# Eighteen weight units instead of seventeen held ahead of an expert stage, and tokens gathered in plain fp32

## The chip, the cores and the metric

The kernel runs on one core of one Trainium2 chip. The metric is the device time of one launch in microseconds (us), the median of three runs. Engines are named as in the profile: PE (TensorE matmul), PEld (its weight loads), DVE (VectorE), ACT (ScalarE), POOL (GpSimd) and SP (SyncE, which here issues the weight DMAs).

## What is computed

Two transformer blocks over 256 tokens of width 1024. The first has a linear recurrence mixer, an attention mixer and two feed-forward layers; the second has two attentions, an output projection and a mixture of experts. Only the last part matters here:

```python
x = x + g1[:, None, :] * (merged @ w_out[l])
h2 = rmsnorm(x, norm2_g[l]) * (1.0 + sc2[:, None, :]) + sh2[:, None, :]
y_ffn = hierarchical_moe(h2, ...)   # 4 groups of 8 experts, the 2 best of one group per token
x = x + g2[:, None, :] * y_ffn
return rmsnorm(x, final_g)
```

Each of the 32 experts has a gate and an up matrix of 1024x512 and a down matrix of 512x1024, all fp32: 6 MB an expert, 192 MB in all.

## The kernel before

**Tiling.** The 256 tokens lie in two tiles of 128 (`t` = 0, 1). Weights come in units of 1 MB; `Stream` (class at L68) issues their DMAs on SP in the order of use into a pool of 17 ring tiles (`RING`). A unit can be loaded only when the matmuls on the unit that had its ring tile before are done. In the early layers a unit is split into a high and a low fp32r part, so that it holds three ring tiles; expert units are used raw, as plain fp32, and hold one. When the last split (of the output projection `bo`) is issued, `ahead` becomes `RING` and the expert units run as far ahead as tiles come free.

**Output projection and router.** `out_proj("bo", ...)` makes four sums `acc[t][nh]` (token tile, half of the columns). For each one `after_mix` adds it to the residual `xres` and sums its squares, and one tick later `later()` transposes it on PE (`pT`), scales it on DVE (`hg`) and multiplies it by the router's weights (`lg`, 8 PE records). Once both halves of a token tile are there, `route(t)` finds group and experts with a chain of small DVE instructions. Also there, `xrH` and `xrL`, the normed tokens as a high and a low fp32r part of 1024 columns, are made with ACT, DVE (t = 0) and POOL (t = 1). They fill four tiles of the `t4` pool (8 tiles of 128x1024). `warm(n)` are n PE matmuls whose result nobody reads. After the last `route`, `pos` (PE) counts places, `place` (DVE) is the slot of each token in its experts, and `selection(m)` writes a 0/1 matrix `sel` for four experts of 64 slots each.

**Gather.** `gathered(sel, half)` fetches the tokens of four experts by matmul: for each of four column chunks four fp32r matmuls of 256 columns (high and low part, two token tiles). Two evictions per PSUM tile, on DVE and on ACT, apply scale and shift and give `xs`.

**Expert loop.** `q` runs over 16 pairs of experts. The unit order is gate 0, up 0, gate 1, down 0, up 1, gate 2, down 1, up 2 and so on, four units each, so that unit numbers 0 to 191 follow from it: unit 17 is the second of up 1, unit 20 the first of gate 2, unit 37 the second of down 2. `half_in` multiplies two units (one for each expert of the pair), which run side by side on two column halves of PE; both become free at its end. `down_products(q-1)` stands between gate q and up q, `scatter` (`comb`) returns results to the residual. A selection serves two pairs; at odd q one half is gathered ahead of up q and one at the end (at q = 3 both at the end). At the end of even q, `places` makes `sT` from `sel` and from the token weights `wtr`. `token_weights()` (softmax over groups and experts, on ACT and DVE) is written at the end of q = 0; the scheduler of the tile library may move instructions ahead within an engine unless they are pinned (`k.pin`, `keep_in_program_order`).

Of the kernel before, what the change touches and what calls it, by code (L numbers as in the profile page):

```python
# [65 lines left out]


class Stream:  # L68

    def __init__(self, k, units):
        self.k = k
        self.units = units
        self.raws = {}
        self.parts = {}
        self.loaded = 0
        self.done = 0
        self.pos = 0
        self.ahead = AHEAD  # L80
        self.most = 2
        self.end = 2 * max(i + 1 for i, u in enumerate(units) if u[4])
        self.plan = []
        self.gated = {}

    def load(self, upto):
        k = self.k
        while self.loaded < min(upto, len(self.units)):
            name, srcs, kc, cols, _ = self.units[self.loaded]
            t = k.big(F32, f"w{self.loaded}")  # L90
            v = t[:, : kc * cols].rearrange("p (k n) -> p k n", k=kc)
            for k0, k1, ap in srcs:
                k.nc.sync.dma_start(v[:, k0:k1, :], ap)
            self.raws[self.loaded] = v
            self.loaded += 1

    def pump(self, upto=None):
# [5 lines left out]
        while self.pos < min(end, 2 * len(self.units)) and (upto is not None or n < self.most):  # L103
# [20 lines left out]
            if self.pos == self.end:  # L124
                self.ahead = RING
                self.load(self.done + self.ahead)
# [310 lines left out]
def two_blocks_kernel(ctx, tc, A, out, stop=None):  # L437
# [66 lines left out]

    def out_proj(prefix, yT, each):

        acc = [[None, None], [None, None]]
        for nh in range(2):
            W = st.take(f"{prefix}0{nh}")
            for t in range(2):  # L510
                acc[t][nh] = k.ps("acc")
                k.tok_mm(acc[t][nh], yT, range(4), t, W, True, False)
                tick()
        Ws = [st.take(f"{prefix}1{nh}") for nh in range(2)]
        for t in range(2):
            for nh in range(2):
                k.tok_mm(acc[t][nh], yT, range(4, 8), t, Ws[nh], False, True)
                each(t, nh, acc[t][nh])
                tick()
# [626 lines left out]
    def merged_T(nh, t, m):  # L1146
        pT = k.ps("mT")
        for i in range(4):
            nc.tensor.transpose(pT[:, i * P : (i + 1) * P], m[:, i * P : (i + 1) * P], k.ident)
# [28 lines left out]
    k.row("b_router", br)  # L1178
    xrH, xrL = ([k.t4(F32R, "xr" + n) for t in range(2)] for n in "HL")
    sh2 = modT[:, 24:32]  # L1180
# [56 lines left out]
    def after_mix(t, nh, p):  # L1237
# [10 lines left out]
        def later():  # L1248
            pT = k.ps("pT")
            for i in range(4):  # L1250
                c = 4 * nh + i
                nc.tensor.transpose(pT[:, i * P : (i + 1) * P], xres[:, t, c * P : (c + 1) * P], k.ident)
            hg, g = k.t2(name="hg"), geff[2][:, 4 * nh : 4 * nh + 4]
# [3 lines left out]
            if nh == 0:  # L1257
                lT[t] = k.ps("lg")
            else:
                xv = xres[:, t, :].rearrange("p (n c) -> p c n", c=8)  # L1260
                hv, lv = (x[t].rearrange("p (c n) -> p c n", c=8) for x in (xrH, xrL))
                nc.scalar.activation(hv, xv, AF.Copy, scale=r)
                if t == 0:
                    nc.vector.scalar_tensor_tensor(lv, xv, r, hv.bitcast(F32), op0=ALU.mult, op1=ALU.subtract)
                    yield 1
                else:
                    warm(5)
                    xn = k.t4(name="xn")
                    nv = xn.rearrange("p (c n) -> p c n", c=8)
                    for h in range(2):  # L1270
                        c = slice(4 * h, 4 * h + 4)
                        nc.scalar.activation(nv[:, c], xv[:, c], AF.Copy, scale=r)
                        nc.gpsimd.tensor_tensor(lv[:, c], nv[:, c], hv[:, c].bitcast(F32), op=ALU.subtract)
            pl = lT[t]
# [9 lines left out]

        routed.append(spawn(later(), 1))

    out_proj("bo", mT, after_mix)
    if stop == "mix2":
# [21 lines left out]
    def token_weights():  # L1310

        ng, gs, ejunk, e1, den, w1 = cut(2), cut(2), cut(2, 4), cut(2), cut(2), cut(2)
        nc.vector.tensor_scalar(ng, gtop[:, :, 0], -1.0, None, op0=ALU.mult)
        for t in range(2):
            nc.scalar.activation(ejunk[:, t, :], lg[:, t, 0:4], AF.Exp, bias=ng[:, t : t + 1], accum_out=gs[:, t : t + 1])
        nc.vector.tensor_tensor(e1, etop[:, :, 1], etop[:, :, 0], op=ALU.subtract)
        nc.scalar.activation(e1, e1, AF.Exp)
        nc.vector.scalar_tensor_tensor(den, e1, 1.0, gs, op0=ALU.add, op1=ALU.mult)
# [19 lines left out]
    def selection(m):  # L1338
# [6 lines left out]
        return sel  # L1345

    def gathered(sel, half):

        xs = k.t4(name="xs").rearrange("p (c s) -> p c s", c=4)
        for c2 in range(2):  # L1350
            p = k.ps("xs")
            for i in range(2):
                c = 4 * half + 2 * c2 + i
                n = 0
                for x in (xrH, xrL):
                    for t in range(2):
                        k.mm(p[:, i * 256 : (i + 1) * 256], x[t][:, c * P : (c + 1) * P], sel[:, t], i == 0 and n == 0, i == 1 and n == 3, True)
                        n += 1
            for i in range(2):
                c = 4 * half + 2 * c2 + i  # L1360
                pv, o = p[:, i * 256 : (i + 1) * 256], xs[:, 2 * c2 + i, :]
                if i:
                    nc.scalar.activation(o, pv, AF.Identity, scale=geffP[:, c : c + 1], bias=shP[:, c : c + 1])  # L1363
                else:
                    nc.vector.tensor_scalar(o, pv, geffP[:, c : c + 1], shP[:, c : c + 1], op0=ALU.mult, op1=ALU.add)  # L1365
        return xs

    def places(q, sel):
# [128 lines left out]
    def overflow():  # L1497
# [10 lines left out]
        for c in range(8):  # L1508
            for t in range(2):
                for h, x in enumerate((xrH, xrL)):  # L1510
                    k.mm(pT[:, t * P : (t + 1) * P], x[t][:, c * P : (c + 1) * P], conr("ident"), t == 0 and h == 0, t == 1 and h == 1, True)
            nc.vector.tensor_scalar(h2T[c // 4][:, c % 4, :], pT[:, 0:256], geffP[:, c : c + 1], shP[:, c : c + 1], op0=ALU.mult, op1=ALU.add)
# [173 lines left out]
```

## Time and profile before

| | |
|---|---|
| median of 3 runs | 1266.68 us (1266.67 to 1267.15) |
| the profiled execution, its own time | 1267.75 us |
| its span | 1266.1 us |
| PE busy | 1225.0 us (97%) |
| DVE, ACT, POOL busy | 719.3, 493.1, 74.7 us |
| HBM traffic | 362.96 MB, mean 287 GB/s |

A busy share of PE here counts matmuls as pipelined, with modelled ends, so 97% doesn't say that PE was the bound everywhere. The span in 40 slices, each of 31.65 us, tells two regimes apart: up to slice 25 the DMA rate wanders between 115 and 319 GB/s, and from slice 26 on (822.9 us) it stands at 420 to 422 GB/s until the last slice.

### The profile page before, as it was taken

How to read it: one execution, taken by the hardware profiler on the slowest of the kernel's cores; microseconds unless marked ns; L12 is line 12 of the kernel's file. 1: busy time of each engine (PE TensorE's matmuls, PEld its weight loads, DVE VectorE, ACT ScalarE, POOL GpSimd, SP SyncE). 2: the span in 40 equal slices, each digit the busy share in tenths (PEclk: the TensorE clock that was granted, in tenths of full speed). 3: DMA queues.
4: the chain of work that ended last, by engine and by line, in shares of the span. 5: the costliest groups of instructions: out<-in, count | busy, mean ns of one | idle time of the engine just before them, and what ended most of it. 6: DMA issues, size and time to landing. Idle time of an engine off the chain costs nothing. (4 is left out here: it accounts for less than half of the span.)

```text
span 1266.1 us, 15923 instructions
## 1 busy us (share of the span) xinstructions
PE 1225.0 (97%) x6247; PEld 852.3 (67%) x6247; DVE 719.3 (57%) x1188; ACT 493.1 (39%) x847; POOL 74.7 (6%) x94
## 2 busy tenths in 40 slices
PE   6999999999999999999999999999999999998996
PEld 6988888998897888898777887543444444343432
DVE  6888669766565866977877785322333322222233
ACT  6956535445676643445566632310110101010101
POOL 4000000000131000100100100000000000000001
PEclk9999999999999999999999999999999999999999
DMA  9756686774334878765635557799999999999995
GB/s 319 262 200 233 235 303 241 244 241 151 117 134 167 282 241 290 237 229 170 218 115 172 188 207 304 286 421 421 420 421 421 421 421 420 422 421 421 421 420 211
DMA packets 121951, 362.96 MB, mean 287 GB/s; under 512 B 6289, under 2 KB 33681, under 8 KB 97809
## 3 DMA queue, kind: packets, MB, share of 16 engines
q1 hardware_dynamic: 121584, 361.39, 75.5%
q8 instruction: 50, 0.82, 0.3%
q10 hardware_dynamic: 288, 0.52, 0.1%
q14 instruction: 29, 0.23, 0.0%
HBM read 360.84 MB, written 1.05 MB: 286 GB/s over the span
## 5 line engine op out<-in xcount | busy, mean ns | idle before, releaser
L242 PE MATMUL down<-w,hidT 128*64 128x512 f32 x512 | 123.1, 595 | 9.5 <-DMA w<-in_w_down_dram 9.5
L242 PE MATMUL up<-w,xs 128*64 128x512 f32 x512 | 122.4, 597 | 5.1 <-DMA w<-in_w_up_dram 5.0
L242 PE MATMUL gate<-w,xs 128*64 128x512 f32 x512 | 116.7, 598 | 0.0
L1424 DVE SCALAR_TENSOR_TENSOR down<-down,wsl,g 128x512 f32<-128x512 f32 x30 | 22.8, 759 | 145.3 <-PE down L242 143.7
L242 PEld LDWEIGHTS down<-w,hidT 128*64 128x64 f32 x512 | 41.4, 137 | 84.9 <-issue 59.6
L242 PEld LDWEIGHTS up<-w,xs 128*64 128x64 f32 x512 | 39.4, 136 | 72.8 <-issue 58.4
L1569 ACT ACTIVATE hid<-gate 128x512 f32<-128x512 f32 x16 | 9.6, 597 | 180.8 <-PE gate L242 180.8
L242 PEld LDWEIGHTS gate<-w,xs 128*64 128x64 f32 x512 | 34.0, 136 | 59.8 <-issue 58.1
L523 DVE TENSOR_TENSOR xres<-comb,xres 128x512 f32<-128x512 f32 x64 | 41.3, 686 | 44.8 <-PE comb L242 44.8
L710 DVE SCALAR_TENSOR_TENSOR adacc<-w,csil,adacc 128x512 f32<-128x512 f32 x84 | 65.2, 777 | 1.3
L1425 ACT CAST oH<-down 128x512 fp32r<-128x512 f32 x30 | 17.6, 587 | 123.7 <-DVE down L1424 123.7
L1363 ACT ACTIVATE xs<-xs,modP,geffP 128x256 f32<-128x256 f32 x32 | 18.1, 564 | 80.4 <-DVE xs L1365 80.4
L1582 DVE TENSOR_TENSOR hid<-up,hid 128x512 f32<-128x512 f32 x16 | 11.1, 692 | 63.8 <-PE up L242 50.4
L778 DVE SCALAR_TENSOR_TENSOR sg<-tb,rs,sg 128x512 f32<-128x512 f32 (+1 forms) x24 | 16.9, 705 | 52.1 <-PE tb L242 52.1
L1405 DVE COPY hidT<-hidT 128x512 f32<-128x512 f32 x16 | 11.1, 692 | 53.1 <-PE hidT L245 53.1
L269 ACT ACTIVATE junk<-xres 128x512 f32<-128x512 f32 x28 | 17.7, 631 | 55.0 <-DVE xres L523 52.7
L714 POOL TENSOR_TENSOR adL<-adacc,adH 128x512 fp32r<-128x512 f32 x12 | 20.0, 1666 | 311.0 <-ACT adH L713 311.0
L764 ACT CAST hH<-hT 128x512 fp32r<-128x512 f32 (+1 forms) x24 | 13.2, 551 | 46.2 <-PE hT L761 46.1
L242 PE MATMUL xs<-sel,xrH 128*128 128x256 f32 x128 | 27.7, 297 | 2.9 <-DVE sel L1342 2.5
L523 DVE TENSOR_TENSOR xres<-acc,xres 128x512 f32<-128x512 f32 x20 | 13.8, 691 | 28.8 <-PE acc L242 28.8
L242 PEld LDWEIGHTS comb<-oH,sT 128*128 128x128 f32 x62 | 11.6, 187 | 26.6 <-issue 24.3
L1479 POOL TENSOR_TENSOR out<-xres,fg 128x512 f32<-128x512 f32 x2 | 2.5, 1272 | 454.5 <-DVE xres L523 454.5
(1270 smaller groups left out, 3367.0 us busy)
## 6 DMA issues: line engine op xcount, KB each, us to landing
w<-in_w_gate_dram SPq DMA_DIRECT2D x64, 1024.0 KB, 19.8
w<-in_w_up_dram SPq DMA_DIRECT2D x64, 1024.0 KB, 19.8
w<-in_w_down_dram SPq DMA_DIRECT2D x60, 1024.0 KB, 19.8
w<-in_ffn_w_in_dram SPq DMA_DIRECT2D x32, 1024.0 KB, 6.6
w<-in_w_ada_dram SPq DMA_DIRECT2D x24, 1024.0 KB, 5.1
w<-in_w_in_dram SPq DMA_DIRECT2D x20, 1024.0 KB, 5.0
w<-in_ffn_w_out_dram SPq DMA_DIRECT2D x16, 1024.0 KB, 6.6
w<-in_ffn_w_in_dram SPq DMA_DIRECT2D x16, 768.0 KB, 5.4
```

Of the source, the lines that this page charges most:

```text
L242: self.pinned(self.nc.tensor.matmul(out, lhsT, rhs, start=start, stop=stop, skip_group_check=skip))
L269: self.nc.scalar.activation(junk[:, : src.shape[-1]], src, AF.Square, scale=scale, accum_out=acc)
L523: nc.vector.tensor_tensor(xres[:, t, s], p, xres[:, t, s], op=ALU.add)
L710: nc.vector.scalar_tensor_tensor(acc, raws[kh][:, i, :], c, acc, op0=ALU.mult, op1=ALU.add)
L714: nc.gpsimd.tensor_tensor(aL, acc, aH.bitcast(F32), op=ALU.subtract)
L764: nc.scalar.copy(hv, pv)
L778: nc.vector.scalar_tensor_tensor(h, p[:, :fw], rs[t], h, op0=ALU.mult, op1=ALU.mult)
L1363: nc.scalar.activation(o, pv, AF.Identity, scale=geffP[:, c : c + 1], bias=shP[:, c : c + 1])
L1405: nc.vector.tensor_copy(hT, p)
L1424: nc.vector.scalar_tensor_tensor(p, p, ws, gates["g2"][:, s], op0=ALU.mult, op1=ALU.mult)
L1425: nc.scalar.copy(oH, p)
L1582: nc.vector.tensor_tensor(hv, hidden_order(q, p), hv, op=ALU.mult)
```

## The change

It does five things.

1. `xrH` and `xrL` and the instructions that made them are gone. The first gather reads `xres` itself, with a selection `selr` that is scaled by each token's reciprocal norm; the later ones read `xc`, an fp32 copy of the scaled tokens, made by two ACT instructions of 1024 columns. Both are plain fp32 matmuls, half as many as before.
2. The first gather is cut by pair: `first_gathered(0)` fetches only the 128 slots of pair 0 ahead of gate 0, `first_gathered(1)` those of pair 1 between gate 0 and up 0.
3. The token tiles freed take an eighteenth expert unit: unit 17 goes into two `t4` tiles (`Halves`) instead of a ring tile, once.
4. The router is pinned in written order (`k.pin` set before `out_proj("bo")`, transposes by `k.turn`), the second half of that projection is cut into pieces of two chunks, and `later()` runs two ticks after its sum. `warm` ahead of the last router product is 2 instead of 5.
5. The start of `token_weights()` is pinned, so that it can't be moved ahead.

```diff
@@ class Stream
+        self.spare = self.end // 2 + RING
+            if self.loaded == self.spare:
+                v = Halves([k.t4(name=f"w{self.loaded}").rearrange("p (k n) -> p k n", k=2) for h in range(2)])
+                for h in range(2):
+                    k.nc.sync.dma_start(v.parts[h], srcs[0][2][:, 2 * h : 2 * h + 2, :])
...
-                self.ahead = RING
+                self.ahead = RING + 1
@@ def out_proj(prefix, yT, each, fine=False)
+                if fine:
+                    k.tok_mm(acc[t][nh], yT, range(4, 6), t, [w[:, 0:2, :] for w in Ws[nh]], False, False)
+                    tick()
+                    k.tok_mm(acc[t][nh], yT, range(6, 8), t, [w[:, 2:4, :] for w in Ws[nh]], False, True)
@@ after_mix, later()
-                nc.tensor.transpose(pT[:, i * P : (i + 1) * P], xres[:, t, c * P : (c + 1) * P], k.ident)
+                k.turn(pT[:, i * P : (i + 1) * P], xres[:, t, c * P : (c + 1) * P])
...
-                nc.scalar.activation(hv, xv, AF.Copy, scale=r)
-                if t == 0:
-                    nc.vector.scalar_tensor_tensor(lv, xv, r, hv.bitcast(F32), op0=ALU.mult, op1=ALU.subtract)
-                    yield 1
-                else:
-                    warm(5)
...
+            elif t == 1:
+                warm(2)
+            yield 1
...
-        routed.append(spawn(later(), 1))
-    out_proj("bo", mT, after_mix)
+        routed.append(spawn(later(), 2))
+    k.pin = True
+    out_proj("bo", mT, after_mix, True)
+    tick()
+    tick()
@@ token_weights()
-        nc.vector.tensor_scalar(ng, gtop[:, :, 0], -1.0, None, op0=ALU.mult)
+        tc.keep_in_program_order(nc.vector.tensor_scalar(ng, gtop[:, :, 0], -1.0, None, op0=ALU.mult))
...
@@ gathered(sel, half)
-                for x in (xrH, xrL):
-                    for t in range(2):
-                        k.mm(p[:, i * 256 : (i + 1) * 256], x[t][:, c * P : (c + 1) * P], sel[:, t], i == 0 and n == 0, i == 1 and n == 3, True)
+                for t in range(2):
+                    k.mm(p[:, i * 256 : (i + 1) * 256], xc[t][:, c, :], sel[:, t].bitcast(F32), i == 0 and t == 0, i == 1 and t == 1, True)
...
+    def first_gathered(q, selr):
+        for half in range(2):
+            p = k.ps("xs")
+            for i in range(4):
+                c = 4 * half + i
+                for t in range(2):
+                    x = xres[:, t, :].rearrange("p (n c) -> p c n", c=8)[:, c, :]
+                    k.mm(p[:, i * P : (i + 1) * P], x, selr[:, t, q * P : (q + 1) * P], i == 0 and t == 0, i == 3 and t == 1, True)
+            for i in range(4):
+                evict(i, xs[half][:, i, q * P : (q + 1) * P], p[:, i * P : (i + 1) * P], 4 * half + i)
@@ expert loop
-    k.pin = True
     sel = selection(0)
-    xs, nxt = [gathered(sel, 0), gathered(sel, 1)], []
+    selr = k.t2(name="selr").rearrange("p (t s) -> p t s", t=2)
+    for t in range(2):
+        tc.keep_in_program_order(nc.vector.tensor_scalar(selr[:, t], sel[:, t].bitcast(F32), rs2[t], None, op0=ALU.mult))
+    xs, nxt = [k.t4(name="xs").rearrange("p (c s) -> p c s", c=4) for half in range(2)], []
+    first_gathered(0, selr)
+    xc = [k.t4(name="xc").rearrange("p (c n) -> p c n", c=8) for t in range(2)]
...
         half_in("gate", q, 1, p)
+        if q == 0:
+            first_gathered(1, selr)
...
         if q == 0:
             token_weights()
+            for t in range(2):
+                nc.scalar.activation(xc[t], xres[:, t, :].rearrange("p (n c) -> p c n", c=8), AF.Copy, scale=rs2[t])
```

The order of instructions at three places, before and now (the line numbers of the changed file are 14 to 33 higher).

DVE before, from the routing of the last tokens to the first gather. `rt` is one tile for all small routing results; L1318 is a step of the token weights, L1342 writes `sel`.

```order
L1235 TENSOR_TENSOR ar<-cst,eu 128x2x32
L1303 TENSOR_TENSOR rt_6755<-ar 128x64
L1304 SCALAR_TENSOR_TENSOR place<-pos_7030,rt_6755 128x64
L1318 SCALAR_TENSOR_TENSOR rt_6755<-rt_6755 128x2
L1342 TENSOR_TENSOR sel_7048<-cst,place 128x256 x2
L1319 RECIPROCAL rt_6755<-rt_6755 128x2
L1329 TENSOR_SCALAR rt_6755<-place 128x64
L1320 TENSOR_TENSOR rt_6755<-rt_6755 128x2
```

DVE now, from the same place up to the token weights (L1327 is their first instruction, L1339 their last; `hid` is the product of gate 0 and up 0):

```order
L1318 SCALAR_TENSOR_TENSOR place<-pos_7019,rt_6751 128x64
L1356 TENSOR_TENSOR sel_7037<-cst,place 128x256 x2
L1584 TENSOR_SCALAR selr_7040<-sel_7037,rs_6914 128x256
L1584 TENSOR_SCALAR selr_7040<-sel_7037,rs_6980 128x256
...
L1613 TENSOR_TENSOR hid_7124<-up_7126,hid_7124 128x512
L1327 TENSOR_SCALAR rt_6751<-rt_6751 128x2
L1330 TENSOR_TENSOR rt_6751<-rt_6751 128x2
L1347 CAST n_over<-over_7169 1x1
L1332 SCALAR_TENSOR_TENSOR rt_6751<-rt_6751 128x2
L1333 RECIPROCAL rt_6751<-rt_6751 128x2
...
L1339 TENSOR_TENSOR wtr<-rt_6751,wtr 128x64
```

The step that stood between `place` and `sel` is behind the product of up 0, with the rest of the token weights.

PE before, from the last router product to gate 0 (32 gather matmuls in all, of which the first two and the last two are shown):

```order
L242 MATMUL lg_6965<-wr,hg_6963 128x40 x4
L242 MATMUL acc_6840<-w155H_6831,mL_6559 128x512
L1252 MATMUL pT_6989<-cst,xres 128x128 x4
...
L242 MATMUL xs_7052<-sel_7048,xrH_6750 128x256
L242 MATMUL xs_7052<-sel_7048,xrH_6751 128x256
...
L242 MATMUL xs_7086<-sel_7048,xrL_6752 128x256
L242 MATMUL xs_7086<-sel_7048,xrL_6753 128x256
L242 MATMUL gate_7097<-w_1045_6661,xs_7051 64x512
```

PE now, from there to gate 1:

```order
L261 MATMUL acc_6836<-w155H_6827,mL_6559 128x512
L261 MATMUL lg_6969<-wr,hg_6967 128x40 x4
L264 MATMUL pT_6987<-cst,xres 128x128 x4
...
L261 MATMUL xs_7058<-selr_7040,xres 128x128 x8
L261 MATMUL gate_7073<-w_1045_6661,xs_7043 64x512
...
L261 MATMUL xs_7098<-selr_7040,xres 128x128 x8
L261 MATMUL xs_7111<-selr_7040,xres 128x128 x8
L261 MATMUL up_7126<-w_1061_6773,xs_7043 64x512
...
L261 MATMUL over_7169<-cr,rt_6751 1x1
L264 MATMUL sT_7174<-cst,sel_7037 128x128 x2
L261 MATMUL sT_7174<-wtr,sel_7037 128x2 x4
```

The last `acc` matmuls now all stand ahead of that router product, 16 gather matmuls stand ahead of gate 0 and 16 ahead of up 0, and the `sT` matmuls that read `wtr` stand where they were.

SP before, the first expert units:

```order
L93 DMA w_1045_6661<-in_w_gate_dram 128x2048
L93 DMA w_1046_6663<-in_w_gate_dram 128x2048
L93 DMA w_1048_6683<-in_w_gate_dram 128x2048
L93 DMA w_1055_6737<-in_w_gate_dram 128x2048
L93 DMA w_1065_6777<-in_w_up_dram 128x2048
```

SP now:

```order
L112 DMA w_1045_6661<-in_w_gate_dram 128x2048
L112 DMA w_1046_6663<-in_w_gate_dram 128x2048
L112 DMA w_1048_6683<-in_w_gate_dram 128x2048
L105 DMA w_1083_6870<-in_w_up_dram 128x1024
L105 DMA w_1084_6871<-in_w_up_dram 128x1024
L112 DMA w_1055_6737<-in_w_gate_dram 128x2048
```

The two halves of unit 17 (`w_1083`, `w_1084`) are issued early, between the third and the fourth unit of gate 0.

## Rows read from the trace of the kernel before

**Rows 1.** The page's span in 40 slices: DMA rate.

```profile
GB/s 319 262 200 233 235 303 241 244 241 151 117 134 167 282 241 290 237 229 170 218 115 172 188 207 304 286 421 421 420 421 421 421 421 420 422 421 421 421 420 211
```

**Rows 2.** Stretches: length, busy PE, PEld, DVE, ACT, POOL, granted PE clock, DMA share, GB/s.

```profile
800.00:802.00 2.00, 1.93 (x8) 1.81 (x9) 1.41 (x10) 0.24 (x1) 0.00 (x0) 0.57 0.61 250
802.00:804.00 2.00, 2.00 (x13) 2.00 (x12) 0.75 (x3) 0.56 (x1) 0.00 (x0) 0.58 0.00 0
805.00:810.00 5.00, 5.00 (x27) 2.09 (x27) 0.97 (x2) 2.48 (x4) 0.00 (x0) 1.00 0.00 0
810.00:815.00 5.00, 5.00 (x26) 1.72 (x24) 0.00 (x0) 0.60 (x1) 0.00 (x0) 1.00 0.91 326
```

**Rows 3.** Timeline of SP, DMA issues (units 17 and 18; unit 37): start, us, operation.

```profile
809.41 1.07 SPq L93 DMA_DIRECT2D w<-in_w_up_dram  x2
...
852.84 0.33 SPq L93 DMA_DIRECT2D w<-in_w_down_dram  x1
```

**Rows 4.** Timeline around the router: start us, us, engine, line, operation [idle before <-releaser].

```profile
776.16 0.39 PE L242 MATMUL acc<-w155H,mH 128*128 128x512 f32 x1
776.39 0.39 PE L242 MATMUL acc<-w155L,mH 128*128 128x512 f32 x1
...
785.92 2.24 DVE L1264 SCALAR_TENSOR_TENSOR xrL<-xres,rs,xrH 128x1024 fp32r<-128x1024 f32 x1 [1.20 <-ACT xrH L1262]
...
789.18 1.08 PE L242 MATMUL lg<-wr,hg 128*128 128x40 f32 x8 [1.31 <-DVE hg L1254]
...
791.35 0.66 PE L1252 MATMUL pT<-cst,xres 128*128 128x128 f32 x4 [0.78 <-DVE xres L523]
...
796.87 0.22 DVE L1304 SCALAR_TENSOR_TENSOR place<-pos,rt 128x64 f32<-128x64 f32 x1 [0.56 <-PE pos L242]
798.08 0.28 ACT L1315 ACTIVATE rt<-lg,rt 128x4 f32<-128x4 f32 x1
798.86 0.73 DVE L1318 SCALAR_TENSOR_TENSOR rt<-rt 128x2 f32<-128x2 f32 x1 [1.76 <-ACT rt L1317]
799.51 0.75 DVE L1342 TENSOR_TENSOR sel<-cst,place 128x256 fp32r<-128x256 f32 x2
800.08 0.88 PE L242 MATMUL xs<-sel,xrH 128*128 128x256 f32 x2 [2.46 <-DVE sel L1342]
...
801.18 0.24 ACT L1324 CAST wtr<-rt 128x64 fp32r<-128x64 f32 x1 [2.36 <-DVE rt L1323]
805.73 7.09 PE L242 MATMUL gate<-w,xs 128*64 128x512 f32 x32
```

**Rows 5.** Timeline of PE in the first block: plain fp32 matmuls `pg` and what follows.

```profile
54.88 3.62 PE L242 MATMUL pg<-rec,w 128*128 128x256 f32 x16
58.15 0.47 PE L242 MATMUL pf<-xH,w9H 128*128 128x256 f32 x1
```

**Rows 6.** Timeline of DVE and PE where q = 0 ends.

```profile
819.83 0.69 DVE L1582 TENSOR_TENSOR hid<-up,hid 128x512 f32<-128x512 f32 x1 [13.44 <-PE over L242]
819.93 0.58 PE L242 MATMUL sT<-wtr,sel 128*128 128x2 f32 x4
```

**Rows 7.** Timeline of PE in the expert loop, gates of q = 5, 6, 7 and 15 among it.

```profile
927.99 3.65 PE L242 MATMUL gate<-w,xs 128*64 128x512 f32 x16
...
942.62 0.50 PE L242 MATMUL xs<-sel,xrH 128*128 128x256 f32 x2
...
944.71 3.65 PE L242 MATMUL up<-w,xs 128*64 128x512 f32 x16
...
954.07 0.40 PE L242 MATMUL xs<-sel,xrH 128*128 128x256 f32 x2
...
956.07 3.65 PE L242 MATMUL gate<-w,xs 128*64 128x512 f32 x16
...
981.18 3.65 PE L242 MATMUL gate<-w,xs 128*64 128x512 f32 x16
...
1217.62 3.65 PE L242 MATMUL gate<-w,xs 128*64 128x512 f32 x16
```

More of the change, by code (lines that the diff above doesn't have):

```diff
@@ L65, with __init__, __getitem__ @@
 CR_W = 128 * len(CR)
+class Halves:
+    def __init__(self, parts):
+        self.parts = parts
+    def __getitem__(self, key):
+        p, i, n = key
+        return self.parts[i // 2][p, i % 2, n]
 class Stream:
@@ L89, in load @@
             name, srcs, kc, cols, _ = self.units[self.loaded]
+            if self.loaded == self.spare:
+                v = Halves([k.t4(name=f"w{self.loaded}").rearrange("p (k n) -> p k n", k=2) for h in range(2)])
+                for h in range(2):
+                    k.nc.sync.dma_start(v.parts[h], srcs[0][2][:, 2 * h : 2 * h + 2, :])
+                self.raws[self.loaded] = v
+                self.loaded += 1
+                continue
             t = k.big(F32, f"w{self.loaded}")
@@ L503, in tok_block, with out_proj @@
                 tick()
-    def out_proj(prefix, yT, each):
+    def out_proj(prefix, yT, each, fine=False):
         acc = [[None, None], [None, None]]
@@ L516, in out_proj @@
             for nh in range(2):
-                k.tok_mm(acc[t][nh], yT, range(4, 8), t, Ws[nh], False, True)
+                if fine:
+                    k.tok_mm(acc[t][nh], yT, range(4, 6), t, [w[:, 0:2, :] for w in Ws[nh]], False, False)
+                    tick()
+                    k.tok_mm(acc[t][nh], yT, range(6, 8), t, [w[:, 2:4, :] for w in Ws[nh]], False, True)
+                else:
+                    k.tok_mm(acc[t][nh], yT, range(4, 8), t, Ws[nh], False, True)
                 each(t, nh, acc[t][nh])
@@ L1148, in merged_T @@
         for i in range(4):
-            nc.tensor.transpose(pT[:, i * P : (i + 1) * P], m[:, i * P : (i + 1) * P], k.ident)
+            k.turn(pT[:, i * P : (i + 1) * P], m[:, i * P : (i + 1) * P])
         pv = pT.rearrange("p (c t) -> p c t", c=4)
@@ L1178, in two_blocks_kernel @@
     k.row("b_router", br)
-    xrH, xrL = ([k.t4(F32R, "xr" + n) for t in range(2)] for n in "HL")
     sh2 = modT[:, 24:32]
@@ L1258, in later @@
                 lT[t] = k.ps("lg")
-            else:
-                xv = xres[:, t, :].rearrange("p (n c) -> p c n", c=8)
-                hv, lv = (x[t].rearrange("p (c n) -> p c n", c=8) for x in (xrH, xrL))
-                nc.scalar.activation(hv, xv, AF.Copy, scale=r)
-                if t == 0:
-                    nc.vector.scalar_tensor_tensor(lv, xv, r, hv.bitcast(F32), op0=ALU.mult, op1=ALU.subtract)
-                    yield 1
-                else:
-                    warm(5)
[L1268 to L1273, printed above, removed]
+            elif t == 1:
+                warm(2)
+            yield 1
             pl = lT[t]
@@ L1345, in selection, with evict @@
         return sel
+    def evict(i, o, pv, c):
+        if i % 2:
+            nc.scalar.activation(o, pv, AF.Identity, scale=geffP[:, c : c + 1], bias=shP[:, c : c + 1])
+        else:
+            nc.vector.tensor_scalar(o, pv, geffP[:, c : c + 1], shP[:, c : c + 1], op0=ALU.mult, op1=ALU.add)
     def gathered(sel, half):
@@ L1353, in gathered @@
                 c = 4 * half + 2 * c2 + i
-                n = 0
-                for x in (xrH, xrL):
-                    for t in range(2):
-                        k.mm(p[:, i * 256 : (i + 1) * 256], x[t][:, c * P : (c + 1) * P], sel[:, t], i == 0 and n == 0, i == 1 and n == 3, True)
-                        n += 1
-            for i in range(2):
[L1360 to L1365, printed above, removed]
-        return xs
+                for t in range(2):
+                    k.mm(p[:, i * 256 : (i + 1) * 256], xc[t][:, c, :], sel[:, t].bitcast(F32), i == 0 and t == 0, i == 1 and t == 1, True)
+            for i in range(2):
+                evict(i, xs[:, 2 * c2 + i, :], p[:, i * 256 : (i + 1) * 256], 4 * half + 2 * c2 + i)
+        return xs
+    def first_gathered(q, selr):
[8 more added lines that the diff above has]
+                evict(i, xs[half][:, i, q * P : (q + 1) * P], p[:, i * P : (i + 1) * P], 4 * half + i)
     def places(q, sel):
@@ L1509, in overflow @@
             for t in range(2):
-                for h, x in enumerate((xrH, xrL)):
-                    k.mm(pT[:, t * P : (t + 1) * P], x[t][:, c * P : (c + 1) * P], conr("ident"), t == 0 and h == 0, t == 1 and h == 1, True)
+                k.mm(pT[:, t * P : (t + 1) * P], xc[t][:, c, :], k.ident, t == 0, t == 1, True)
             nc.vector.tensor_scalar(h2T[c // 4][:, c % 4, :], pT[:, 0:256], geffP[:, c : c + 1], shP[:, c : c + 1], op0=ALU.mult, op1=ALU.add)
@@ L1566, in two_blocks_kernel @@
         half_in("gate", q, 1, p)
+        if q == 0:
+            first_gathered(1, selr)
+            selr = None
         hid = k.t2(name="hid")
```

6 lines of the change are left out of this document (3 added, 3 removed).

## The prediction

> **What bounds the kernel now.** I read the span in slices first. From slice 26 on (822.9 us) the DMA rate stands at 420 to 422 GB/s to the end [rows 1]: the expert stage streams at what the DMA engines give, and a unit of 1 MB takes 1048.6 KB / 421 GB/s = 2.49 us. A stage on such a stream ends a fixed tail after its last unit, so the question is when the stream starts and whether it ever breaks.
>
> The stretches show the start. Between 805 and 810 us nothing moves: 17 units are loaded, all ring tiles are full. In the next 5 us 326 GB/s are moved [rows 2], that is 5 x 326 / 421 = 3.9 us at full rate, so the first byte of the next unit (number 17) came at 811.1. Its issue stands at 809.41 [rows 3], behind the first half of gate 0, which begins at 805.73 [rows 4] and takes some 3.5 us (half of its 7.09). Refilling an empty queue thus costs 1.7 us beyond the issue.
>
> The timeline ahead of gate 0 shows what sets its start. The last transposes (791.35) are late because the router product at 789.18 waited 1.31 us for DVE, which had been held by `xrL` (2.24 us from 785.92), with the last `acc` matmuls queued behind it. Then `place` ends at 797.09, yet `sel` only starts at 799.51, since the token-weight step L1318 stands in between and waited for ACT. PE starts the gather at 800.08 [rows 4].
>
> In the loop PE isn't far from being the bound. From gate 5 to gate 7 (927.99 to 981.18) it never waits, and two pairs take 53.2 us; the stream needs 24 x 2.49 = 59.8 us for them. From gate 7 to gate 15 it takes 236.4 us instead of 4 x 53.2 = 212.8 [rows 7]: 23.7 us, nearly all waits for weights, are what PE has to spare until then.
>
> **The change, part by part: up to gate 0.** The router now runs in written order. From the first matmul on the last weight tile (776.16) PE has 36 `acc` matmuls at 0.23 us from start to start, three groups of transposes (0.66) and three router products (1.08) to issue ahead of the last transposes [rows 4]: 8.3 + 2.0 + 3.2 = 13.5 us with the modelled ends of the last two, about 12.5 without. That puts the last transposes at 788.7 to 789.7 instead of 791.35; I take 2.3 us earlier, close to the two waits that the rows list (1.31 + 0.78). The DVE chain from there to the end of `place` (5.74 us) stays. The router products themselves are unchanged, and the removed conversions were hidden otherwise.
>
> Behind `place`, `sel` follows at once: 0.75 us for both halves, and two `selr` of the same size, for which I take 0.65 (0.75 at most). The gather starts at 797.09 - 2.3 + 0.75 + 0.65 + 0.05 = 796.2, against 800.08: 3.9 us earlier. It now has 16 plain fp32 matmuls of 128 columns, two records each. Sixteen records of 256 columns take 3.27 us from 54.88 to 58.15 [rows 5], 0.204 each, so 0.102 for half the columns is the lower bound; 1.08 / 8 = 0.135 from a router product, whose 40 columns leave only the weight loads [rows 4], is the upper. I take 0.115, nearer the first since these rows stream 128 columns: 32 x 0.115 = 3.7 us. Gate 0 starts at 799.9, **5.8 us earlier** than 805.73.
>
> **Behind gate 0.** `first_gathered(1)` adds the same **3.7 us** on PE ahead of up 0. The token weights, before done in the gap ahead of the first gather, now start behind the product `hid` of up 0. Nothing hides them: the `sT` matmuls on PE wait for `wtr`, gate 1 queues behind these, and the ring tiles of gate 1 behind gate 1. From the start of `hid` at 819.83: 0.69 for `hid`, 0.2 for the first small step, 0.78 for the exponentials (798.08 to 798.86), 2.56 from L1318 to the end of the cast (801.42) less the 0.7 of `sel` that stood in it [rows 4], and 0.25 for the low part: 3.8 us, against 0.1 from `hid` to the `sT` matmul before [rows 6]. **+3.7 us**; 3.0 if L1318's 0.73 was itself a wait, 4.2 with gaps between the small steps.
>
> At odd q each half gather becomes 8 matmuls of 256 columns, 3.27 us by the `pg` rows [rows 5], for 2.09 and 2.00 [rows 7]. The two halves of q = 1 add **2.5 us** (2.2 to 3.0).
>
> The two ACT instructions that make `xc` are needed only at the gather of q = 1; the gates cover them.
>
> **What the eighteenth unit is worth.** Its 2.49 us fit into the 5 us and more in which no data moves [rows 2], so 18 units are there when gate 0 starts. But the ring behind it still has 17 tiles: unit 37 takes the tile of unit 20, as before, whatever unit 17 lies in. Before, unit 37 is issued at 852.84 [rows 3] and could start at 854.6 (1.7 us later), while the stream reaches it at 811.1 + 20 x 2.49 = 860.9: 6.4 us of slack. Now its release moves by -5.8 + 3.7 + 3.7 + 2.5 = +4.1, while the unbroken stream would reach it 5.8 + 2.5 = 8.3 us earlier. The slack is overdrawn, the stream breaks at unit 37 (a little also at 22 and 26) and goes on 4.1 - 6.4 = **-2.3 us** against before. Of the lead that the unit gives, this takes all.
>
> [...]
>
> After that the stream has slack (at later units the release gains 6.6 us on it per two pairs before, some 4 now), and the tail is unchanged. PE's own end: -5.8 + 3.7 + 3.7 + 14 x 1.2 = +18.4 of 23.7 to spare, -5.3, so it stays 3 us behind the stream. **Sum: -2.3 us.** The profiled execution, 1267.75 with its span of 1266.1, would become 1265.4. It stands 1.07 above the median, so the median goes from 1266.68 to 1264.4. With every bound to one side the sum runs from -4.1 to +0.5.
>
> **Rivals.** *The stream never breaks* (the token weights or the second gather lie beside something after all): the whole lead counts, -5.8 - 2.5 = -8.3, 1258.4. For it: a break needs 8.3 + 4.1 - 6.4 = 6.0 us to be right about, and part of it may fail. Against it: PE, DVE and ACT all work in order and the chain is in the listed order.
>
> [...]
>
> *PE becomes the bound (slower).* If the fp32 gather pays for weight loads that the `pg` rows hide, a half takes X instead of 3.27 us, and PE's end moves by -5.3 + 14 (X - 3.27). It decides from X = 3.5 on and is over +2.5 from X = 3.83; 0.06 us more per record (X = 4.23) gives +8.1, 1274.8. Against it: 16 records of this very kind in 3.27 us.
>
> *The pinning brings nothing*: the last transposes stay at 791.35, and 2.3 us of the gain go: 1266.7.
>
> **How the numbers follow.** The forecast has 0.45, the unbroken stream 0.20, the clock 0.18, PE as the bound 0.08, the pinning 0.09. A measurement here tells about 0.2% from no change, 2.5 us. The forecast lies just inside of that, so a bit under half of it counts as faster: 0.21 + 0.20 + 0.02 = 0.43. Slower is PE as the bound, and ends of the clock and of the forecast: 0.12. The rest, 0.45, is the same. The range goes from 1258.8, short of the unbroken stream, to 1267.9, past the forecast's upper bound with the lower clock; it leaves out PE as the bound and half of the unbroken stream.
>
> **What would show it.** Gate 0 near 800; PE idle some 3.5 us behind up 0, until `wtr`; in the DMA rate a dip about 26 us and again about 57 us behind the start of gate 0; PE waits for weights of a few us in all, in place of more than 20; the gather at 3.3 us a half. [...]

## The result, and the profile after

The changed kernel takes 1274.37 us (median of 4 runs, 1273.36 to 1275.44) against 1266.68: a ratio of 1.0062, 95% interval 1.0049 to 1.0074. It is **slower by 7.7 us** (0.6%, and the interval lies above 1), where 2.3 us less were forecast. The profiled execution took 1275.44 us, its span is 1273.8. PE is busy 1246.3 us of it, 21.3 more than before.

The DMA rate over 40 slices, from the page:

```profile
GB/s 318 260 198 231 243 309 240 240 223 166 101 132 198 271 242 282 246 224 179 196 125 173 169 278 320 254 356 374 420 421 421 421 421 421 421 421 421 421 420 219
```

Before, slices 26 and 27 had 421 and 421 [rows 1]; now they have 356 and 374. The stream of weights breaks there, and from slice 28 on it runs at the old rate to the end. Where it breaks is seen in stretches (length, busy PE, PEld, DVE, ACT, POOL, granted PE clock, DMA share, GB/s):

```profile
820.00:825.00 5.00, 5.00 (x27) 1.58 (x24) 0.05 (x1) 1.03 (x1) 0.00 (x0) 1.00 0.50 149
825.00:830.00 5.00, 2.31 (x12) 2.08 (x12) 3.04 (x16) 1.01 (x6) 0.00 (x0) 0.73 1.00 419
830.00:835.00 5.00, 5.00 (x16) 1.74 (x18) 1.40 (x5) 0.00 (x0) 0.00 (x0) 0.59 0.66 275
835.00:840.00 5.00, 5.00 (x26) 1.77 (x24) 0.69 (x1) 0.00 (x0) 0.00 (x0) 1.00 0.64 208
865.00:870.00 5.00, 5.00 (x26) 1.77 (x24) 0.69 (x1) 0.00 (x0) 0.00 (x0) 1.00 0.63 210
...
1256.00:1258.00 2.00, 2.00 (x10) 0.81 (x6) 0.92 (x3) 0.04 (x1) 0.00 (x0) 1.00 0.94 354
1258.00:1260.00 2.00, 2.00 (x10) 0.52 (x9) 1.67 (x3) 0.58 (x1) 0.00 (x0) 1.00 0.08 32
```

The last stretches of the kernel before, for comparison:

```profile
1248.00:1250.00 2.00, 2.00 (x10) 0.75 (x7) 0.92 (x2) 0.00 (x0) 0.00 (x0) 1.00 0.95 362
1250.00:1252.00 2.00, 2.00 (x11) 0.69 (x10) 2.00 (x4) 0.62 (x1) 0.00 (x0) 1.00 0.19 73
```

The last bytes land near 1250.4 before (2 x 73 / 362 = 0.4 us into the last stretch) and near 1258.2 now (2 x 32 / 354 = 0.2). The stream ends **7.8 us later**, as much as the kernel does. The last break is the one at 865 to 870, and its cause stands in SP's timeline:

```profile
866.97 0.80 SPq L112 DMA_DIRECT2D w<-in_w_down_dram  x2
```

This is unit 37, issued at 852.84 before [rows 3]: 14.1 us later, since the matmuls of gate 2 on unit 20, whose tile it takes, come 14.1 us later. PE's timeline says which steps these 14.1 us are:

```profile
775.92 0.39 PE L261 MATMUL acc<-w155H,mH 128*128 128x512 f32 x1
...
788.28 0.66 PE L264 MATMUL pT<-cst,xres 128*128 128x128 f32 x4
...
795.12 7.88 PE L261 MATMUL xs<-selr,xres 128*128 128x128 f32 x32 [0.66 <-DVE selr L1584]
802.93 7.09 PE L261 MATMUL gate<-w,xs 128*64 128x512 f32 x32
809.94 7.92 PE L261 MATMUL xs<-selr,xres 128*128 128x128 f32 x32
817.79 7.09 PE L261 MATMUL up<-w,xs 128*64 128x512 f32 x32
...
828.05 1.06 PE L261 MATMUL sT<-wtr,sel 128*128 128x2 f32 x4 [2.69 <-ACT wtr L1338]
...
830.24 5.55 PE L261 MATMUL gate<-w,xs 128*64 128x512 f32 x16
835.72 0.66 PE L264 MATMUL hidT<-cst,hid 128*128 128x128 f32 x4
...
846.75 3.72 PE L261 MATMUL xs<-sel,xc 128*128 128x256 f32 x16
850.40 3.65 PE L261 MATMUL up<-w,xs 128*64 128x512 f32 x16
...
859.75 3.62 PE L261 MATMUL xs<-sel,xc 128*128 128x256 f32 x16
863.29 1.94 PE L261 MATMUL gate<-w,xs 128*64 128x512 f32 x8
```

The same places of the kernel before, where they did not stand in the rows above:

```profile
812.65 7.04 PE L242 MATMUL up<-w,xs 128*64 128x512 f32 x32
...
821.09 3.65 PE L242 MATMUL gate<-w,xs 128*64 128x512 f32 x16
824.67 0.66 PE L245 MATMUL hidT<-cst,hid 128*128 128x128 f32 x4
...
835.71 0.50 PE L242 MATMUL xs<-sel,xrH 128*128 128x256 f32 x2
...
837.81 3.65 PE L242 MATMUL up<-w,xs 128*64 128x512 f32 x16
...
847.17 0.40 PE L242 MATMUL xs<-sel,xrH 128*128 128x256 f32 x2
...
849.17 1.08 PE L242 MATMUL gate<-w,xs 128*64 128x512 f32 x4
```

Start against start, the way to gate 2 reads:

| step | before | after | difference |
|---|---|---|---|
| start of gate 0 | 805.73 | 802.93 | -2.80 |
| gate 0 to up 0 (with the second first gather) | 6.92 | 14.86 | +7.94 |
| up 0 to gate 1 (token weights) | 8.44 | 12.45 | +4.01 |
| first half of gate 1 | 3.58 | 5.48 | +1.90 |
| gather ahead of up 1 | 2.10 | 3.65 | +1.55 |
| gather ahead of gate 2 | 2.00 | 3.54 | +1.54 |
| **start of gate 2** | 849.17 | 863.29 | **+14.1** |

With the slack of 6.4 us that the prediction read for unit 37, 14.1 - 6.4 = 7.7 us is what the stream should lose. It lost 7.8, and the median 7.7. From the start of gate 2 to the end of the trace it is 416.9 us before (849.17 to 1266.1) and 410.5 now (863.29 to 1273.8).

### The profile page after: what moved, and what is told of

Read it like the earlier page. It is cut to its first block, busy times and chain, and to the rows that moved or that the text cites. A ratio compares the mean times of both kernels' runs of the same rounds, so it can differ in the third digit from the quotient of the medians.

```text
span 1273.8 us, 15992 instructions
## 1 busy us (share of the span) xinstructions
PE 1246.3 (98%) x6276; PEld 868.6 (68%) x6276; DVE 720.1 (57%) x1193; ACT 494.3 (39%) x851; POOL 72.0 (6%) x92
## 5 line engine op out<-in xcount | busy, mean ns | idle before, releaser
L261 PE MATMUL up<-w,xs 128*64 128x512 f32 x512 | 116.0, 596 | 0.0
L261 PE MATMUL down<-w,hidT 128*64 128x512 f32 x512 | 113.7, 593 | 0.0
L261 PEld LDWEIGHTS down<-w,hidT 128*64 128x64 f32 x512 | 36.7, 137 | 72.1 <-issue 67.0
L261 PEld LDWEIGHTS up<-w,xs 128*64 128x64 f32 x512 | 34.9, 137 | 68.3 <-issue 67.9
L1363 ACT ACTIVATE xs<-xs,modP,geffP 128x256 f32<-128x256 f32 (+1 forms) x36 | 19.5, 541 | 117.3 <-DVE xs L1365 117.3
L261 PE MATMUL xs<-sel,xc 128*128 128x256 f32 x224 | 51.2, 382 | 2.0 <-PEq L1631 2.0
L261 PEld LDWEIGHTS xs<-sel,xc 128*128 128x128 f32 x224 | 41.9, 190 | 13.0 <-issue 4.1
L1365 DVE TENSOR_SCALAR xs<-xs,geffP,modP 128x256 f32<-128x256 f32 (+1 forms) x36 | 18.5, 513 | 45.9 <-PE xs L261 43.8
L288 ACT ACTIVATE junk<-xres 128x512 f32<-128x512 f32 x28 | 17.7, 631 | 56.6 <-DVE xres L547 53.5
## 6 DMA issues: line engine op xcount, KB each, us to landing
w<-in_w_down_dram SPq DMA_DIRECT2D x60, 1024.0 KB, 17.7
```

The lines of the kernel that those rows point to most:

```text
L261: self.pinned(self.nc.tensor.matmul(out, lhsT, rhs, start=start, stop=stop, skip_group_check=skip))
L288: self.nc.scalar.activation(junk[:, : src.shape[-1]], src, AF.Square, scale=scale, accum_out=acc)
```

## The experiments

Two questions were open after this reading. Why does a record of the first gathers take 7.88 / 32 = 0.246 us, where 0.115 was expected? And is the end set by the stream, through the ring tiles, or by PE itself? PE waits for no weights any more in the whole expert stage (its list of waits names none, that of the kernel before 14.5 us), which speaks for PE. Times of the kernel before beside these runs are 1266.95 to 1267.12 us; one run alone (the strides) had 1266.07 beside it.

**Neighbouring columns.** In `first_gathered`:

```diff
-  x = xres[:, t, :].rearrange("p (n c) -> p c n", c=8)[:, c, :]
+  x = xres[:, t, c * P : (c + 1) * P]
```

The experts get other features than they should by this; only the times are of use.

> The changed kernel, but the two first gathers (q = 0 and 1) take as stationary operand 128 neighbouring columns of the fp32 sums instead of every eighth one. This hands the experts other features (the values are no longer those of the reference), with the same number and size of instructions. Theory: a weight load that reads every eighth fp32 element (a stride of 32 bytes) takes 0.336 us where one of neighbouring columns takes 0.190, and that is what made a record 0.245 us. Then a record takes 0.11 to 0.135 us here, each first gather 3.5 to 4.3 us instead of 7.8, gate 0 starts at 798.6 to 799.5, and the end comes some 8 us sooner: 1266 to 1267. Rival: an fp32 matmul of 128 columns costs 0.245 us a record in itself, or the lower clock made it so; then both gathers stay at 7.8 us and the time at 1274.

Measured: 1266.48 us, ratio 0.9998 (0.9989 to 1.0008), that is 8.1 us less than the changed kernel by the ratios. The weight loads of the first gathers by tile (ns min/median/max, first and last start, shape), in the changed kernel:

```profile
L261 PEld LDWEIGHTS xs<-selr,xres x64: 312/336/338, 795.1 to 817.3; 128*128 128x128 f32 x64
```

and here:

```profile
L261 PEld LDWEIGHTS xs<-selr,xres x64: 186/192/193, 793.7 to 807.9; 128*128 128x128 f32 x64
```

The first of them in the timeline of this run:

```profile
793.71 3.81 PE L261 MATMUL xs<-selr,xres 128*128 128x128 f32 x32 [0.68 <-DVE selr L1584]
797.45 7.09 PE L261 MATMUL gate<-w,xs 128*64 128x512 f32 x32
```

3.74 us for 32 records are 0.117 each, what the prediction took. The edit changes the stride alone, so the stride made them 0.246. The rival (the size, or the clock) falls. The clock is ruled out a second time by the second first gather of the changed kernel, which took 7.85 us (809.94 to 817.79) at a granted clock of 1.00, and by the run without the eighteenth unit (below): its first one took 7.82 us (794.37 to 802.19) at 1.00, that of the changed kernel 7.81 at .66 between 795 and 800. The stretch in the changed kernel, then in that run, with its gather:

```profile
795.00:800.00 5.00, 4.88 (x21) 4.91 (x21) 0.97 (x4) 0.25 (x1) 0.00 (x0) 0.66 1.03 426
795.00:800.00 5.00, 5.00 (x23) 5.00 (x22) 0.82 (x2) 0.61 (x2) 0.00 (x0) 1.00 0.92 385
794.37 7.89 PE L261 MATMUL xs<-selr,xres 128*128 128x128 f32 x32 [0.68 <-DVE selr L1584]
```

**Other strides.** The same line with strides of two and four elements, since between 0.192 us at 4 bytes and 0.336 at 32 the load can step up or grow with the stride:

```diff
-  x = xres[:, t, :].rearrange("p (n c) -> p c n", c=8)[:, c, :]
+  m = (2, 4)[q]
+  x = xres[:, t, :].rearrange("p (n c) -> p c n", c=m)[:, c % m, c // m * P : (c // m + 1) * P]
```

> The changed kernel, with the first gather's stationary operand at every second fp32 element (8 bytes) for q = 0, and at every fourth (16 bytes) for q = 1, instead of every eighth (other features, not those of the reference). [...] Rival (the load grows with the stride step by step): some 0.21 and 0.26 us a load, 4.5 and 5.8 us a gather.

The weight loads by tile, in the stretch of the first gather (every second element) and in that of the second (every fourth):

```profile
L261 PEld LDWEIGHTS xs<-selr,xres x32: 194/196/197, 794.3 to 797.9; 128*128 128x128 f32 x32
...
L261 PEld LDWEIGHTS xs<-selr,xres x32: 308/329/329, 805.3 to 812.5; 128*128 128x128 f32 x32
```

0.196 us at 8 bytes, 0.329 at 16, 0.336 at 32 (above): a step between 8 and 16 bytes, not a slope. The gathers took 3.94 and 7.66 us, where a slope gives 4.5 and 5.8, and the one run 1270.44. The rival (a slope) falls. What makes the step isn't shown.

**Token weights early.**

```diff
     first_gathered(0, selr)
+    token_weights()
...
         if q == 0:
-            token_weights()
```

> The changed kernel, with the token-weight step emitted right behind the first gather, ahead of gate 0, instead of behind up 0. Theory: the wait of the sT matmuls for wtr (2.7 us in the list, 3.95 from the end of up 0 to gate 1 beyond what it was) and the fall of the clock to .59 behind it (gate 1's first half 5.55 instead of 3.58 us) both go, so gate 1 starts 4 us sooner, its first half takes 3.6, and since nothing between there and the ring tiles of unit 37 waits for anything else, the end comes 6 us sooner: 1268 to 1269. Rival: the end is set by PE's steady work alone or by a transfer that starts at a fixed time, and the 6 us turn into a wait elsewhere: 1273 to 1275. Second rival: the clock falls all the same (it comes from the first gather), only 4 us are won: 1270.5.

Measured: 1269.60 us, ratio 1.0019 (1.0009 to 1.0028), 5.4 us less than the changed kernel by the ratios. Gate 1 in PE's timeline:

```profile
826.42 3.65 PE L261 MATMUL gate<-w,xs 128*64 128x512 f32 x16
```

and the stretch around it:

```profile
825.00:830.00 5.00, 5.00 (x30) 2.40 (x28) 2.72 (x9) 0.00 (x0) 0.00 (x0) 1.00 1.01 426
```

Up 0 starts at 818.05 here, so gate 1 follows it after 8.37 us (12.45 in the changed kernel), at a clock of 1.00. The time is 0.6 above the upper end of what was expected; the clock of 1.00 speaks against the second rival, whose 1270.5 is not far off. PE's list has no wait for weights left in this run, so part of the 6 us may have met PE's own end; that was not taken apart.

**The wait filled.** In `places`, between the transposes of `sel` and the matmuls with `wtr`:

```diff
+        if q == 0:
+            warm(12)
```

> The changed kernel with 12 idle-work matmuls of 512 columns (some 2.6 us) put on PE into the wait of the sT matmuls for wtr; the wait itself stays. Theory: gate 1's first half took 5.55 us instead of 3.58 because the clock fell while PE stood still; kept busy, PE keeps 1.00, that half takes 3.6 us again and the end comes 2 us sooner, 1272 to 1272.7. Rival: the clock falls for another reason (the slow first gathers ahead of it), 1274 to 1275.

Measured: 1272.23 us, ratio 1.0042 (1.0028 to 1.0057), 2.5 us less by the ratios. PE's timeline and the stretch behind the wait:

```profile
824.22 2.98 PE L261 MATMUL warm<-cr 128*128 128x512 f32 x12
...
828.47 3.65 PE L261 MATMUL gate<-w,xs 128*64 128x512 f32 x16
825.00:830.00 5.00, 5.00 (x28) 3.36 (x28) 3.54 (x17) 0.86 (x6) 0.00 (x0) 1.00 1.00 421
```

The wait is still there (up 0 starts at 816.88, gate 1 at 828.47, 11.59 us later), but the stretch 825 to 830 now has a clock of 1.00 instead of .73, and gate 1's first half its 3.65 us. So the fall of the clock behind up 0 came from PE standing still there, and cost some 2 us. In the traces it is 15.17 us from the start of up 0 to the end of that half, 17.93 in the changed kernel: 2.76 us.

**fp32r gathers from q = 3 on.**

```diff
...
+        if q == 2:
+            xhl[:] = [k.t4(F32R, "xr").rearrange("p (c n) -> p c n", c=8) for i in range(4)]
+            for h in range(2):
+                for t in range(2):
+                    c = slice(4 * h, 4 * h + 4)
+                    nc.scalar.copy(xhl[t][:, c], xc[t][:, c])
+                    nc.vector.tensor_tensor(xhl[2 + t][:, c], xc[t][:, c], xhl[t][:, c].bitcast(F32), op=ALU.subtract)
```

with `gathered` reading the four tiles of `xhl`, once they are there, against `sel`.

> The changed kernel, with the gathers from q = 3 on as they were before (two fp32r parts, made from the scaled copy at q = 2); the two first gathers, the token-weight wait and the gather of q = 1 stay as changed. Theory (stream): the end is set by the DMA stream, which the late release of ring tiles by the first gathers, the wait and the clock breaks at units up to 37; the 12 later half gathers, 1.5 us longer each, only use up what PE had to spare. Then the time stays at 1273.5 to 1275 and PE waits for weights again, some 15 to 20 us in all. Rival (PE): the 21.6 us that the plain fp32 gathers add to PE set the end; then 12 x 1.5 = 18 us go from PE, and the end falls to where the stream would be, 1267 or less.

Measured: 1272.61 us, ratio 1.0050 (1.0033 to 1.0067), 0.9 us below what was expected and far from the rival's 1267. With 18 us taken from PE the time is 1.5 us shorter by the ratios, which the two intervals can't tell from nothing. From the start of gate 2 to the end of the trace it is 409.8 us (861.00 to 1270.8), 410.5 in the changed kernel: 0.7 us. The rest of the difference between the two traces lies ahead of gate 2, where the edit changes nothing. PE's waits, in the list by releaser (in total, times, longest):

```profile
PE down L261 <- DMA w<-in_w_down_dram: 6.4, 7, 1.3
PE up L261 <- DMA w<-in_w_up_dram: 2.6, 2, 1.3
```

The waits for weights come back. The list names 9.0 us of them, where 15 to 20 were expected, but by starts there are more. Two pairs take 53.2 us here without a wait and 56.25 in the changed kernel, which is 18.4 us over six such steps; so of the 409.8 us, 409.8 - (410.5 - 18.4) = 17.7 are waits. The stream sets the end here, 6.3 us later than in the kernel before: by itself it makes most of the loss. PE's long gathers only used up what PE had to spare. In the changed kernel the two limits lie within some 1.5 us of each other.

**Without the eighteenth unit.**

```diff
-        self.spare = self.end // 2 + RING
+        self.spare = -1
...
-                self.ahead = RING + 1
+                self.ahead = RING
```

> The changed kernel without the eighteenth unit (the ring alone, as before). Theory (the stream is broken where it reaches unit 37, whose tile is that of unit 20 with or without the eighteenth unit): the unit buys only a longer standstill there, so the time stays at 1274, within 1 us, and the DMA rate has a longer gap at gate 0 and a shorter one around 835 us. Rival: the unit's 2.49 us count, 1276.5 to 1277.

Measured: 1273.97 us, ratio 1.0058 (1.0041 to 1.0074), the same as with it; the rival's 1276.5 would be 1.0075, just outside. The stretches:

```profile
800.00:805.00 5.00, 5.00 (x24) 3.13 (x25) 0.82 (x2) 4.60 (x4) 0.00 (x0) 1.00 0.03 11
835.00:840.00 5.00, 5.00 (x26) 1.72 (x24) 0.32 (x1) 1.70 (x2) 0.00 (x0) 1.00 0.95 359
```

Less moves ahead of gate 0 (11 GB/s, 48 with the unit), more at 835 to 840 (359, 208 with it). What the unit loads early, the stream waits for later.

**The scaled copy first.** Both repairs in another form: `xc` is made by ACT as soon as a token half has its norm, the first gathers read it and `sel`, and the token weights follow the first gather.

```diff
...
             r = rs2[t] = k.rsqrt(ss2[t])
+            xc[t] = k.t4(name="xc").rearrange("p (c n) -> p c n", c=8)
+            tc.keep_in_program_order(nc.scalar.activation(xc[t], xres[:, t, :].rearrange("p (n c) -> p c n", c=8), AF.Copy, scale=r))
...
-                    x = xres[:, t, :].rearrange("p (n c) -> p c n", c=8)[:, c, :]
-                    k.mm(p[:, i * P : (i + 1) * P], x, selr[:, t, q * P : (q + 1) * P], i == 0 and t == 0, i == 3 and t == 1, True)
+                    x = xc[t][:, c, :]
+                    k.mm(p[:, i * P : (i + 1) * P], x, sel[:, t, q * P : (q + 1) * P].bitcast(F32), i == 0 and t == 0, i == 3 and t == 1, True)
...
     first_gathered(0, sel)
+    token_weights()
...
```

> The changed kernel with both repairs, in another form: the scaled copy xc is made by ScalarE as soon as each token half has its norm (ahead of the router's last part, where ScalarE is idle), the first gathers take their stationary operand from it (neighbouring columns, and sel itself instead of the scaled selr), and the token-weight step follows the first gather. By the theory (stride, wait, clock): the first gather starts behind sel, at 794.8, takes 3.5 to 4.3 us, gate 0 at 798.4 to 799.2, the second 3.5 to 4.3, no wait for wtr. The release of unit 20's tile comes 0.5 us sooner than in the kernel before, the stream runs 6.9 us ahead of it: 1259 to 1261, faster than both kernels. Rival (PE is the bound): nearly the same, 1260, but then without waits for weights. Rival (an fp32 record costs 0.245 us anyway): 1267 to 1269.

Measured: **1260.11 us**, ratio 0.9943 (0.9926 to 0.9959), faster than both kernels (by 0.6% against the kernel before). PE's timeline:

```profile
773.98 0.39 PE L261 MATMUL acc<-w155H,mH 128*128 128x512 f32 x1
...
792.58 3.92 PE L261 MATMUL xs<-sel,xc 128*128 128x128 f32 x32
...
796.55 7.09 PE L261 MATMUL gate<-w,xs 128*64 128x512 f32 x32
```

From the first matmul on the last weight tile to gate 0 it takes 22.6 us; the kernel before took 29.6 [rows 4], the changed one 27.0. No wait for weights is left on PE. That is the sign named for the rival, PE as the bound, and its time is the same, so this run doesn't tell which of the two ends comes later; the next one takes work off PE.

**The same with fp32r gathers from q = 3 on** (the edit shown above):

> The version with the scaled copy first and the token weights early, with fp32r gathers from q = 3 on besides. In the version without these PE never waited for weights and its last unit of down began 3.9 us behind the last landing, where the kernel before has 3.2. Theory (the end is tied: PE's own end only 0.7 us behind the stream's): 18 us less of PE give back those 0.7 at most, 1259 to 1260.5. Rival (PE is the bound): several us, 1256 or less.

Measured: 1260.50 us, ratio 0.9951 (0.9934 to 0.9967). Nothing comes out of 18 us less of PE, so the stream ends as late as PE did. The stretch in which the stream reaches unit 37:

```profile
850.00:855.00 5.00, 5.00 (x28) 1.74 (x26) 1.17 (x2) 0.00 (x0) 0.00 (x0) 1.00 0.69 229
```

It still breaks there. In all it loses less: slices 26 and 27 of the page have 423 and 385 GB/s, 356 and 374 in the changed kernel.

**The tiles of the eighteenth unit given to fp32r parts.** The fp32r parts are made at q = 0 instead of q = 2, and the ring is alone, as in the run without the unit:

> The same, but the tiles of the eighteenth unit go to the two fp32r parts, made during gate 0, so that the gather of q = 1 is short too (2.05 instead of 3.6 us a half); no eighteenth unit. Theory: the release of unit 20's tile comes 7.0 - 3.8 = 3.2 us sooner than in the kernel before and the slack there is 6.4 + 3.2 = 9.6 us, more than the 7.0 by which the stream starts sooner; it doesn't break, and the end comes 7.0 us ahead of the kernel before, 1259 to 1260.5, with no eighteenth unit at all. Rival (the eighteenth unit is worth its 2.49 us): 1262 to 1263.

Measured: **1259.17 us**, ratio 0.9941 (0.9925 to 0.9958). The stretches from 810 us on:

```profile
810.00:815.00 5.00, 5.00 (x26) 1.58 (x22) 0.00 (x0) 0.21 (x1) 0.00 (x0) 1.00 0.94 351
815.00:835.00 20.00, 20.00 (x106) 8.77 (x106) 7.02 (x16) 2.90 (x5) 0.00 (x0) 1.00 1.01 425
835.00:870.00 35.00, 35.00 (x172) 14.88 (x170) 11.44 (x20) 2.90 (x5) 0.00 (x0) 1.00 1.01 422
```

Beyond a dip at 810 to 815 (351 of 421 GB/s, 0.8 us) the stream does not break, at unit 37 neither, and that with seventeen units. The intervals of the last three versions overlap, so they can't be ranked; all three are faster than the kernel before, by 0.5 to 0.6%.

## Why the prediction was wrong

**Up to the gather it held.** The last transposes come 12.4 us after the first matmul on the last weight tile, 15.2 before: 2.8 us earlier where 2.3 were taken. The gather starts at 795.12, 5.0 us earlier on the clock of the trace (3.9 taken, so 1.1 to the good). So the rival in which the pinning brings nothing falls.

**The step that failed** is the price of a record of the first gathers: "0.102 for half the columns is the lower bound; 1.08 / 8 = 0.135 from a router product, whose 40 columns leave only the weight loads [rows 4], is the upper. I take 0.115". It measured 0.246, far outside both bounds. Both rows were of stationary operands of neighbouring columns, and the diff says in plain sight that this one takes every eighth element. With neighbouring columns 0.117 was measured, so the sum was right for another instruction. This one number stands in two terms: the first gather took 7.8 us instead of 3.7, so that gate 0 came 2.8 us earlier instead of 5.8, and ahead of up 0 the second added 7.94 instead of 3.7. (The bounds of all terms to one side give -4.5 to +0.7 rather than the -4.1 to +0.5 of the prediction; neither comes near +7.7.)

**The token-weight wait** was sized nearly right. In the run that fills it, at a clock of 1.00, gate 1 starts 11.59 us after up 0, 8.44 before: 3.15 us, where 3.7 were taken. The other 0.86 of the 4.01 in the table belong to the clock, since the `sT` matmuls behind the wait ran slower too (2.19 us from the end of the wait to gate 1, 1.32 with the wait filled). **The fall of the clock** is the second step that failed: the sum put it at nothing, the chances gave it 0.18. The range reaches 1267.9 with a price for the lower clock that no run shows. In its place the runs showed this: the fall came, and cost 0.86 + 1.90 = 2.76 in this trace (2.5 by the ratios of the run that fills the wait). PE was busy 2.31 of the 5 us from 825 on, and the granted clock was 0.73 and then 0.59 in the two stretches; with the wait filled it was 1.00 from 825 to 830. The length of a wait alone didn't tell whether the clock falls: in the changed kernel it was .66 between 795 and 800 us behind a wait of only 0.66 us for `selr`, and in the run without the eighteenth unit it stayed at 1.00 behind one of 0.68. That earlier fall cost nothing, since the first gather took as long at either clock (7.81 and 7.82 us).

**The gathers of q = 1** added 3.1 us instead of 2.5. A half takes 3.54 to 3.65 us from start to start, not 3.27. Why these records are slower than those of `pg` is open.

**How these make the time was right.** Five terms are off by +3.0 (gate 0), +4.2 (the second first gather), -0.5 (the wait), +2.8 (the clock) and +0.6 (q = 1), together 10.0 unrounded. The release of unit 20's tile moved by +14.1 instead of +4.1, and -2.3 + 10.0 = +7.7 is the measured difference. The slack of 6.4 us is borne out, to within 0.7 us: from the start of gate 2 on, 416.9 - 410.5 = 6.4, and where the stream breaks and PE waits for weights it is 410.5 too in the version with the scaled copy and fp32r gathers (848.62 to 1259.1) and 409.8 in the changed kernel with such gathers. One reading behind the slack was wrong, without harm to the sum: the first byte does not come 1.7 us after the issue, at 811.1. In half microseconds of the trace before, data moves from 810.0 to 810.5 already, 0.6 to 1.1 us after the issue at 809.41, and the rate then climbs:

```profile
810.00:810.50 0.50, 0.50 (x4) 0.14 (x2) 0.00 (x0) 0.00 (x0) 0.00 (x0) 1.00 0.61 98
812.50:813.00 0.50, 0.50 (x4) 0.14 (x2) 0.00 (x0) 0.11 (x1) 0.00 (x0) 1.00 1.12 475
```

The 1.7 us are what the wait for the first byte and the climb cost together, and that is what the sum needs.

**The rivals.** PE as the bound was the only one on the slower side, and its time, 1274.8, is nearly the one measured, but its mechanism is not what happened. By its own formula a half gather of 3.6 us gives -5.3 + 14 x 0.33 = -0.7, no loss. PE did wait for no weights at all, as it would if it were the bound, and that proves nothing: PE was late by the same 14.1 us, so its own end moved by 14.1 + 12 x 1.55 - 23.7 = +9.0, next to the stream's +7.7. The chain of waits of the changed kernel, all PE and no DMA, could not tell the two apart; taking work off PE could. With 18 us less of PE the waits are back and 6.3 of the 7.7 us remain, so the stream alone makes these; whether the last 1.5 us are PE's is not settled. The unbroken stream did not come with this kernel, and came, with another version, at 1259.2, close to its 1258.4.

**What the eighteenth unit is worth** was forecast as nothing, since the stream breaks at unit 37 with or without it. The run without it bears that out, to within some 2 us.

## What to carry to other kernels

Before a matmul is priced from a row, compare the layout of its operands with that row's, not only size and type: a stationary operand read through a rearranged view cost twice here (0.246 us a record, 0.117 with neighbouring columns). A unit more of prefetch bought nothing here (1274.37 us with it, 1273.97 without), as a later unit waited for the release of a ring tile; ask for the first unit that needs a used tile, and count every step in front of that release. When two limits lie close together, the list of waits may name neither, as here; take work off one and see whether the end moves.

## What was not expected of the hardware

- The weight load of a 128x128 fp32 operand takes 0.192 us at a stride of 4 bytes, 0.196 at 8, 0.329 at 16 and 0.336 at 32; with it a gather of 32 records of 128 columns went from 3.74 to 7.8 us. That the load sets the pace there is argued, not shown by a run of its own: the time is the same at a granted clock of .66 and of 1.00, and it moves with the load in all four strides (3.74, 3.94, 7.66 and 7.81 to 7.85 us).
- A wait of 2.7 us on PE cost as much again in the work behind it in the changed kernel, at a clock of .73 and .59 (gate 1's first half, 16 records of 512 columns, took 5.48 instead of 3.58 us). In four traces with this wait (the changed kernel, neighbouring columns, fp32r gathers from q = 3 on, without the eighteenth unit), up 0 with what follows to the end of that half takes 16.87 to 18.16 us, 15.17 with the wait filled, so the price runs from 1.7 to 3.0 us. Filled with 2.98 us of matmuls that nobody reads, the wait cost nothing beyond itself.
